# One core, two blocks in fp32 halves: GpSimd's two-operand passes on VectorE

## The chip, the cores and the metric

The kernel runs on one core of a Trainium2 chip as a single program. The metric is the device time of one execution in microseconds (us). Before the change the median of three runs is 1876.54 us (1874.93 to 1879.38).

A core has five engines, each with its own in-order stream of instructions, which wait for one another through semaphores: TensorE (PE: matmuls, and PEld: weight loads into the array), VectorE (DVE), ScalarE (ACT), GpSimd (POOL) and SyncE (SP, which here issues the transfers). SBUF is the on-chip memory, PSUM the matmuls' accumulator.

## The reference

One sequence of 256 tokens, 1024 channels, runs through two networks in a row, each of two layers, all in float32.

```python
# first block, per layer l
h = rmsnorm(x, norm1_g[l]) * (1 + sc1) + sh1
x = x + g1 * token_mix(h, ...)       # gated linear recurrence + latent attention, two branch gates
h = rmsnorm(x, norm2_g[l]) * (1 + sc2) + sh2
x = x + g2 * grouped_moe(h, ...)     # 16 experts of width 512, 2 per token
# the recurrence, chunks of 64 tokens, b = cumsum(log f), k = 1 - f
decay = exp(b[t] - b[s])             # t >= s
attn  = sum_d q[t] * decay * k[s]
# second block, per layer i (layer 0: windowed attention, layer 1: short convolution)
h = h + g1 * mixer(modulate(rms_norm(h, norm_mix[i]), sh1, sc1))
h = h + g2 * conv_ffn(modulate(rms_norm(h, norm_ffn[i]), sh2, sc2))   # width 2816
```

## The kernel before, in words

**Halves.** TensorE multiplies float32 in a rounded form (fp32r). To keep the precision, every operand is split into a high part and a rest: `split_to` (L515) has ScalarE copy a weight tile of 128x1024 to `hi` (L516), and VectorE or GpSimd subtract, `lo = w - hi` (L517). `mm3` (L534 to L537) then sends three matmuls per tile of 128x128: high by high, high weight by low activation, low weight by high activation. So a matmul of line L537 cannot start before its `lo` is there. `split_w` (L519) splits a loaded piece of 256 columns as two halves, by default the first `lo` on VectorE and the second on GpSimd (`engs=(V, G)`).

**Stages.** In order of time: token mix of layer 0 (0 to 325 us), its experts (to 603), token mix of layer 1 (to 895), its experts (to 1170), then the second block: windowed attention (to 1335), its feed-forward (to 1552), short convolution (to 1662), its feed-forward (to the end).

**Norms.** `norm_split` (L447) scales the activation with the norm and splits it in `hh` and `hl`. With the norm's scale given as `r`, VectorE makes `w = x * gain * r` (L454) for eight slices of 128x256, ScalarE adds the shift and rounds to `hh` (L458), VectorE takes the rest `hl` (L459). At a stage's start TensorE has nothing to do until these eight steps and the first weight halves are there. Otherwise the scale comes late: L474 multiplies by the gain, L492 by the norm.

**Token mix.** `forget`, `query`, `value`, `gate` (L643 to L712) project and make the recurrence's operands; GpSimd has two products in `query` (L681, L687). `states` transposes L687's result on TensorE (L720). `decays` (L737) makes six tiles `z` of 128x512 for the levels m = 2 to 64: a difference (L745: GpSimd for m = 4, 16, 64, VectorE for the others), two exponentials on ScalarE (L746, L747), and two products of 128x256 (L748 on VectorE, L749 on GpSimd). `recur` multiplies the tiles on TensorE (L765).

**Second block.** The query projections of the windowed attention turn their output by the rotary angles (L1574 to L1578: GpSimd has L1575). In `conv_ffn` the first two weight pieces of each feed-forward are split by GpSimd alone (`engs=(G, G) if g0 + s == 0`, L1776), all others by VectorE.

**What sets the order.** The program is written in one order, and a scheduler orders the instructions of each engine by priority and by its own estimate of when an engine is free. So a change of an engine moves other instructions too, on all engines but SP. `P` and `hlp` are pools of buffers in rotation: a raw weight tile is free for SP's next load when its split is done.

```python
513  def split_to(hi, lo, raw, lo_eng=None): ...
517      (lo_eng or V).tensor_tensor(lo, raw, hi.bitcast(F32), OP.subtract)
535      PE.matmul(ps, wh, ah, ...)      # hi by hi
536      PE.matmul(ps, wh, al, ...)      # hi by lo of the activation
537      PE.matmul(ps, wl, ah, ...)      # lo of the weight by hi
```

Of the kernel before, what the change touches and what calls it, by code (L numbers as in the profile page):

```python
# [108 lines left out]
def tile_kernel(ctx, tc, A, out, dbg=None, stop=None):  # L109
# [336 lines left out]
    def norm_split(x, gn, sh, pp, sp, w, hh=None, hl=None, before=None, late=None, r=None):  # L446

        if r is not None:
            for k in range(KD):
                if hh is None and k % 4 == 3:  # L450
                    G.tensor_tensor(w[k], x[:, k], r, OP.mult)
                    S.activation(w[k], w[k], AF.Identity, scale=gn[:, k:k + 1], bias=sh(k))
                    continue
                V.scalar_tensor_tensor(w[k], x[:, k], gn[:, k:k + 1], r, op0=OP.mult, op1=OP.mult)  # L454
                if hh is None:
                    S.activation(w[k], w[k], AF.Identity, bias=sh(k))
                else:
                    S.activation(hh[:, k], w[k], AF.Identity, bias=sh(k))  # L458
                    V.scalar_tensor_tensor(hl[:, k], w[k], sh(k), hh[:, k].bitcast(F32), op0=OP.add, op1=OP.subtract)  # L459
            return  # L460
# [30 lines left out]
        for k in range(KD):  # L491
            (G if k % 4 == 3 else V).tensor_tensor(w[k], w[k], r, OP.mult)  # L492
            if hh is None:
                S.activation(w[k], w[k], AF.Identity, bias=sh(k))
            else:
                S.activation(hh[:, k], w[k], AF.Identity, bias=sh(k))
                V.scalar_tensor_tensor(hl[:, k], w[k], sh(k), hh[:, k].bitcast(F32), op0=OP.add, op1=OP.subtract)
# [20 lines left out]

    def split_w(raw, hlp, kc, widths=(128, 128), engs=(V, G)):  # L519

        r, at = [], 0
        for i, n in enumerate(widths):
            hi, lo = pair(hlp, (kc, n))
            split_to(hi, lo, raw[:, :, at:at + n], engs[i])
            r.append((hi, lo))
            at += n
        return r
# [40 lines left out]
    def token_mix(l):  # L568
        key = (0, l)
        with ExitStack() as es:  # L570
# [64 lines left out]

            def proj(c0, s, engs=(V, V)):
                if s == 0 and c0 < 1024 and l:
                    engs = (G, G) if c0 else (V, G)
                w = pre.pop() if pre else split_w(load_w(w_in, 0, 8, c0 + 256 * s, 256), hlp, 8, engs=engs)
                return dense2(P, w, h, 8)  # L640
# [28 lines left out]
            def query(s):  # L669
# [10 lines left out]
                r.qi = H()  # L680
                G.tensor_tensor(r.qi, r.q, r.eb, OP.mult)  # L681
                kd = H()
# [3 lines left out]
                S.activation(kd, kd, AF.Exp, scale=-1.0)  # L686
                G.tensor_tensor(kd, kd, r.kk, OP.mult)  # L687
                r.kd = kd
# [48 lines left out]
            def decays(s):  # L737

                r = R[s]
                r.Z = []  # L740
                for m in (2, 4, 8, 16, 32, 64):
                    z = sp.tile([128, 2, T], F32, name=nm("z"), tag="z")
                    zb, bb, kb, qb = (x.rearrange("p h (c t) -> p (h c) t", t=m) for x in (z, r.b, r.kk, r.q))
                    n, mh = 2 * T // m, m // 2
                    (G if m in (4, 16, 64) else V).tensor_tensor(zb, bb, bb[:, :, mh - 1:mh].to_broadcast([128, n, m]), OP.subtract)  # L745
                    S.activation(zb[:, :, :mh], zb[:, :, :mh], AF.Exp, scale=-1.0)  # L746
                    S.activation(zb[:, :, mh:], zb[:, :, mh:], AF.Exp)  # L747
                    V.tensor_tensor(zb[:, :, :mh], zb[:, :, :mh], kb[:, :, :mh], OP.mult)  # L748
                    G.tensor_tensor(zb[:, :, mh:], zb[:, :, mh:], qb[:, :, mh:], OP.mult)  # L749
                    r.Z.append(z)  # L750
# [49 lines left out]
            def latents(s):  # L800
                ps = proj(2048, s, (V, V))
                for x in lat:
# [129 lines left out]
            def branch_gate(n, j):  # L932
                ps = proj(2720 + 1024 * j, n, (V, G))
                x_ = sig[n, j] = H()
# [528 lines left out]
    def win_attention(l, key):  # L1463
        with ExitStack() as es:
# [55 lines left out]
            for i in range(2):  # L1520
                split_to(*wv[i], raw[:, 4 * i:4 * i + 4], G if i else V)
            tc.cur_priority = tc.cur_priority + EARLY
# [3 lines left out]
            for k in range(KD):  # L1526
# [6 lines left out]
                if PAIR:  # L1533
                    (G if k < 4 else V).tensor_tensor(sq, sq, even, OP.add)
                with tc.issue_after(turned.ins):
# [16 lines left out]
            def bc2(x):  # L1552
                return x[:, None, :].to_broadcast([128, 2, T])
# [6 lines left out]
            def head_norm(ps, gcol, turn):  # L1560
# [11 lines left out]
                if turn:  # L1572
                    b_ = sp.tile([128, 2, T], F32, name=nm("rb"), tag="sq")
                    V.tensor_tensor(b_, p2, bc2(sinw), OP.mult)  # L1574
                    G.tensor_tensor(x, x, bc2(cosw), OP.mult)  # L1575
                    V.tensor_tensor(x, x, b_, OP.add)
# [34 lines left out]
            def wq(i):  # L1611
                return split_w(load_w(w_qkv, 0, 8, 256 * i, 256), hlp, 8, engs=(V, V))
            k1 = keys(1, hc)
# [121 lines left out]
    def conv_ffn(l, key):  # L1735
        with ExitStack() as es:
# [31 lines left out]
            for g0 in range(0, nb, 4):  # L1768
                n4 = min(4, nb - g0)
                for s in range(n4 // 2):  # L1770
# [4 lines left out]
                    for j, r in enumerate(rgu):  # L1775
                        ps = dense2(P, split_w(r, hlp, 8, engs=(G, G) if g0 + s == 0 else (V, V)), act(hh, hl), 8)  # L1776
                        y = sp.tile([128, 2, T], F32, name=nm("y"), tag="y")
# [98 lines left out]
```

## Time and profile before

| what | us |
|---|---|
| median of three runs | 1876.54 (1874.93 to 1879.38) |
| the profiled execution | 1876.0 |
| its span, first to last instruction | 1874.2 |
| PE busy in the span | 1727.8 (92%) |
| DVE busy | 1026.2 (55%) |
| ACT busy | 802.4 (43%) |
| POOL busy | 239.9 (13%) |

The profile is of one execution. An engine's busy time is the time in which it had an instruction under way; PE's matmuls overlap a little, and their ends are modelled. "L454 DVE" means line 454 of the kernel, run by VectorE. A number in brackets behind a row of the timeline is the idle time of that engine just before it, with the instruction that ended it. A wait is idle time of an engine, put down to the instruction whose end released it.

### The profile page before, as it was taken

The page shows a single profiled execution, that of the slowest core. Times are in us where ns is not written, and L with a number is a line of the kernel's source. Part 1 is how long each engine was busy: PE and PEld are TensorE (multiplying, and loading weights), DVE is VectorE, ACT ScalarE, POOL GpSimd, SP SyncE. Part 2 cuts the span into 40 slices and gives each one's busy share as a digit, 9 for nine tenths or more (in the row PEclk, how much of TensorE's full clock was granted, in tenths as well). Part 3 has the DMA queues.
Part 4 walks back from the last instruction along what each step waited for, and adds up shares of the span by engine and source line. Part 5 has one row for each costly group of instructions (what it writes and reads, how often), then busy time and mean ns, then how long its engine had stood idle before and what let it go on. Part 6 is the DMA issues. An engine that isn't in the chain of part 4 may idle for free. (4 is left out here: it accounts for less than half of the span.)

```text
span 1874.2 us, 30827 instructions
## 1 busy us (share of the span) xinstructions
PE 1727.8 (92%) x12555; PEld 1307.8 (70%) x12555; DVE 1026.2 (55%) x1838; ACT 802.4 (43%) x1460; POOL 239.9 (13%) x134
## 2 busy tenths in 40 slices
PE   6989998999999799999899988979899999989998
PEld 4777798444444777689444333857799997979998
DVE  4876555222222886555322222887576766678774
ACT  4544553111112553544211112767465554456663
POOL 1320232000000320223000000130200003430000
PEclk8999999899999899999899998999999999999999
DMA  9777894798799566896699997520587736576520
GB/s 319 250 259 258 293 328 158 283 392 318 290 391 368 181 204 240 292 324 216 240 386 392 392 387 260 165 91 1 193 300 272 246 114 202 181 267 228 180 91 23
DMA packets 277952, 467.33 MB, mean 249 GB/s; under 512 B 9282, under 2 KB 138288, under 8 KB 277728
## 3 DMA queue, kind: packets, MB, share of 16 engines
q1 hardware_dynamic: 276720, 462.76, 70.1%
q8 instruction: 143, 2.34, 0.5%
q10 hardware_dynamic: 656, 1.32, 0.2%
q14 instruction: 81, 0.66, 0.1%
q0 software_dynamic: 352, 0.23, 0.0%
HBM read 463.24 MB, written 1.05 MB: 248 GB/s over the span
## 5 line engine op out<-in xcount | busy, mean ns | idle before, releaser
L535 PE MATMUL mm<-hh,hi 128*128 128x256 f32 x1584 | 458.8, 290 | 11.1 <-ACT hh L458 5.7
L536 PE MATMUL mm<-hl,hi 128*128 128x256 f32 x1584 | 454.0, 287 | 9.5 <-DVE hl L459 7.7
L537 PE MATMUL mm<-hh,lo 128*128 128x256 f32 x1584 | 453.5, 286 | 4.6 <-DVE lo L517 4.6
L516 ACT CAST hi<-w 128x1024 fp32r<-128x1024 f32 (+4 forms) x330 | 309.6, 970 | 220.5 <-PE mm L536 178.4
L517 DVE TENSOR_TENSOR lo<-w,hi 128x1024 fp32r<-128x1024 f32 (+4 forms) x264 | 299.7, 1148 | 95.2 <-ACT hi L516 94.9
L517 POOL TENSOR_TENSOR lo<-w,hi 128x1024 fp32r<-128x1024 f32 x66 | 165.1, 2507 | 1275.7 <-ACT hi L516 1275.7
L535 PEld LDWEIGHTS mm<-hh,hi 128*128 128x128 f32 x1584 | 306.5, 194 | 26.2 <-ACT hh L458 8.4
L536 PEld LDWEIGHTS mm<-hl,hi 128*128 128x128 f32 x1584 | 307.0, 194 | 12.3 <-DVE hl L459 8.3
L537 PEld LDWEIGHTS mm<-hh,lo 128*128 128x128 f32 x1584 | 306.5, 193 | 7.8 <-DVE lo L517 5.4
L1194 PE MATMUL ps<-w,xg 128*64 128x512 f32 x512 | 231.7, 606 | 8.1 <-ACT xg L1166 5.7
L1195 PE MATMUL ps<-w,xg 128*64 128x512 f32 x512 | 231.5, 606 | 1.6 <-DMA w<-in_w_up_dram 1.6
L1194 PEld LDWEIGHTS ps<-w,xg 128*64 128x64 f32 x512 | 69.8, 139 | 149.1 <-issue 138.8
L1212 DVE TENSOR_TENSOR gx<-gx,ps 64x512 f32<-64x512 f32 (+1 forms) x35 | 23.4, 669 | 225.7 <-ACT gx L1211 187.1
L1211 ACT ACTIVATE gx<-ps 64x512 f32<-64x512 f32 (+1 forms) x35 | 20.0, 571 | 217.6 <-PE ps L1195 214.7
L1238 PE MATMUL ps<-w,he 128*64 128x512 f32 x240 | 110.7, 600 | 0.0
L1237 PE MATMUL ps<-w,he 128*64 128x512 f32 x240 | 110.0, 599 | 0.2 <-DMA w<-in_w_down_dram 0.2
L370 PE MATMUL ps<-w,crep 128*32 128x512 f32 x768 | 106.1, 605 | 3.4 <-DMA w<-in_ada_w_dram 2.0
L536 PE MATMUL yT<-zl,hi 128*128 128x256 f32 x352 | 99.1, 282 | 0.0
L535 PE MATMUL yT<-zh,hi 128*128 128x256 f32 x352 | 99.1, 281 | 0.0
L537 PE MATMUL yT<-zh,lo 128*128 128x256 f32 x352 | 99.0, 281 | 0.0
L535 PE MATMUL mm<-half,hi 128*128 128x256 f32 x320 | 93.0, 291 | 0.0
L536 PE MATMUL mm<-half,hi 128*128 128x256 f32 x320 | 91.2, 285 | 0.0
(468 smaller groups left out, 3014.5 us busy)
## 6 DMA issues: line engine op xcount, KB each, us to landing
w<-in_ada_w_dram SPq DMA_DIRECT2D x96, 1024.0 KB, 6.9
w<-in_w_gate_dram SPq DMA_DIRECT2D x64, 1024.0 KB, 14.5
w<-in_w_up_dram SPq DMA_DIRECT2D x64, 1024.0 KB, 16.2
w<-in_w_down_dram SPq DMA_DIRECT2D x64, 1024.0 KB, 12.7
w<-in_ffn_w_up_dram SPq DMA_DIRECT2D x44, 1024.0 KB, 5.3
w<-in_w_in_dram SPq DMA_DIRECT2D x36, 1024.0 KB, 8.7
w<-in_ffn_w_down_dram SPq DMA_DIRECT2D x22, 1024.0 KB, 6.8
w<-in_sc_w_in_dram SPq DMA_DIRECT2D x12, 1024.0 KB, 7.3
```

Source lines behind the costliest of these rows:

```text
L370: PE.matmul(ps[32 * g:32 * g + 32], crep[blk][:, 4 * s + g, SLOTS - 1 - i:SLOTS + 31 - i], w[i][s][:, g], start=(i + s == 0), stop=(i == n ...
L516: S.copy(hi, raw)
L517: (lo_eng or V).tensor_tensor(lo, raw, hi.bitcast(F32), OP.subtract)
L535: PE.matmul(ps, wh, ah, start=start, stop=False, skip_group_check=True)
L536: PE.matmul(ps, wh, al, start=False, stop=False, skip_group_check=True)
L537: latest[0] = PE.matmul(ps, wl, ah, start=False, stop=stop, skip_group_check=True).ins
L1194: PE.matmul(ps[0:64], xg[:, k, off:off + SL], wg[k // 4][:, k % 4], start=(k == 0), stop=(k == KD - 1), skip_group_check=True)
L1195: m = PE.matmul(ps[64:128], xg[:, k, off:off + SL], wu[k // 4][:, k % 4], start=(k == 0), stop=(k == KD - 1), skip_group_check=True)
L1211: S.activation(x_, ps[0:64], AF.Silu)
L1212: V.tensor_tensor(x_, x_, ps[64:128], OP.mult)
L1237: PE.matmul(py[0:64], he[:, j], cut(e, j, 0), start=(j == 0), stop=(j == 3), skip_group_check=True)
L1238: m = PE.matmul(py[64:128], he[:, j], cut(e, j, 1), start=(j == 0), stop=(j == 3), skip_group_check=True)
```

## The change

All two-operand passes that GpSimd ran go to VectorE: the 66 splits (L517), 24 products L749, 12 differences L745, four each of L681 and L687, five of L1575, two sums of L1534 and two of the norm's products L492; 119 instructions. GpSimd keeps its transfers. (The branch of `norm_split` that is deleted at L450 to L453 is never taken in this program.)

```diff
@@ norm_split
-                if hh is None and k % 4 == 3:
-                    G.tensor_tensor(w[k], x[:, k], r, OP.mult)
...
-            (G if k % 4 == 3 else V).tensor_tensor(w[k], w[k], r, OP.mult)
+            V.tensor_tensor(w[k], w[k], r, OP.mult)
@@ split_w
-    def split_w(raw, hlp, kc, widths=(128, 128), engs=(V, G)):
+    def split_w(raw, hlp, kc, widths=(128, 128)):
...
-            split_to(hi, lo, raw[:, :, at:at + n], engs[i])
+            split_to(hi, lo, raw[:, :, at:at + n])
@@ token mix: proj, query, decays, gates
-            def proj(c0, s, engs=(V, V)):
-                if s == 0 and c0 < 1024 and l:
-                    engs = (G, G) if c0 else (V, G)
+            def proj(c0, s):
...
-                G.tensor_tensor(r.qi, r.q, r.eb, OP.mult)
+                V.tensor_tensor(r.qi, r.q, r.eb, OP.mult)
...
-                G.tensor_tensor(kd, kd, r.kk, OP.mult)
+                V.tensor_tensor(kd, kd, r.kk, OP.mult)
...
-                    (G if m in (4, 16, 64) else V).tensor_tensor(zb, bb, bb[:, :, mh - 1:mh].to_broadcast([128, n, m]), OP.subtract)
+                    V.tensor_tensor(zb, bb, bb[:, :, mh - 1:mh].to_broadcast([128, n, m]), OP.subtract)
...
-                    G.tensor_tensor(zb[:, :, mh:], zb[:, :, mh:], qb[:, :, mh:], OP.mult)
+                    V.tensor_tensor(zb[:, :, mh:], zb[:, :, mh:], qb[:, :, mh:], OP.mult)
...
-                ps = proj(2720 + 1024 * j, n, (V, G))
+                ps = proj(2720 + 1024 * j, n)
@@ windowed attention
-                split_to(*wv[i], raw[:, 4 * i:4 * i + 4], G if i else V)
+                split_to(*wv[i], raw[:, 4 * i:4 * i + 4])
...
-                    (G if k < 4 else V).tensor_tensor(sq, sq, even, OP.add)
+                    V.tensor_tensor(sq, sq, even, OP.add)
...
-                    G.tensor_tensor(x, x, bc2(cosw), OP.mult)
+                    V.tensor_tensor(x, x, bc2(cosw), OP.mult)
@@ conv_ffn
-                        ps = dense2(P, split_w(r, hlp, 8, engs=(G, G) if g0 + s == 0 else (V, V)), act(hh, hl), 8)
+                        ps = dense2(P, split_w(r, hlp, 8), act(hh, hl), 8)
```

How the instructions move is shown at three places. In the changed kernel the line numbers are lower by four to seven: L450 and L455 are L454 and L459 of before, L513 is L517, L531 to L533 are L535 to L537, L739, L742, L743 are L745, L748, L749, L675, L678, L681 are L681, L684, L687, L700 is L706.

First VectorE at the start of the second block's first feed-forward (about 1336 us), before:

```order
L1690 SCALAR_TENSOR_TENSOR xT<-mm_26129,mod(1, 0)_190,xT 128x256 x2
L454 SCALAR_TENSOR_TENSOR wt_26212<-xT,gf_26210,rnorm 128x256 x2
L454 SCALAR_TENSOR_TENSOR wt_26213<-xT,gf_26210,rnorm 128x256 x2
L459 SCALAR_TENSOR_TENSOR hl_26209<-wt_26212,mod(1, 0)_190,hh_26208 128x256 x2
L459 SCALAR_TENSOR_TENSOR hl_26209<-wt_26213,mod(1, 0)_190,hh_26208 128x256 x2
L454 SCALAR_TENSOR_TENSOR wt_26214<-xT,gf_26210,rnorm 128x256 x2
```

and with the change:

```order
L1684 SCALAR_TENSOR_TENSOR xT<-mm_26129,mod(1, 0)_190,xT 128x256 x2
L513 TENSOR_TENSOR lo_26286<-w_26279,hi_26285 128x1024
L513 TENSOR_TENSOR lo_26290<-w_26279,hi_26289 128x1024
L513 TENSOR_TENSOR lo_26358<-w_26281,hi_26357 128x1024
L450 SCALAR_TENSOR_TENSOR wt_26212<-xT,gf_26210,rnorm 128x256 x2
L450 SCALAR_TENSOR_TENSOR wt_26213<-xT,gf_26210,rnorm 128x256
L455 SCALAR_TENSOR_TENSOR hl_26209<-wt_26212,mod(1, 0)_190,hh_26208 128x256 x2
```

Three of the four splits that POOL ran stand ahead of the norm's steps now; the fourth comes behind all sixteen of them.

Second, VectorE in the decays of token mix layer 1 (about 633 to 645 us), before:

```order
L745 TENSOR_TENSOR z_12725<-half_12511 128x512
L745 TENSOR_TENSOR z_12737<-half_12511 128x512
L745 TENSOR_TENSOR z_12749<-half_12511 128x512
L517 TENSOR_TENSOR lo_12804<-w_12801,hi_12803 128x1024
L676 SCALAR_TENSOR_TENSOR half_12522<-half_12522,half_12583 128x512
L748 TENSOR_TENSOR z_12725<-z_12725,half_12510 128x256
L684 TENSOR_TENSOR half_12592<-half_12511 128x512
L748 TENSOR_TENSOR z_12731<-z_12731,half_12510 128x128x2
```

and with the change:

```order
L670 SCALAR_TENSOR_TENSOR half_12522<-half_12522,half_12583 128x512
L742 TENSOR_TENSOR z_12725<-z_12725,half_12510 128x256
L675 TENSOR_TENSOR half_12590<-half_12522,half_12588 128x512
L678 TENSOR_TENSOR half_12592<-half_12511 128x512
L743 TENSOR_TENSOR z_12725<-z_12725,half_12522 128x256
L742 TENSOR_TENSOR z_12731<-z_12731,half_12510 128x128x2
L743 TENSOR_TENSOR z_12731<-z_12731,half_12522 128x128x2
L681 TENSOR_TENSOR half_12592<-half_12592,half_12510 128x512
```

The product L687 of before, which TensorE's transposes L720 wait for, stands as L681 seven instructions behind L676 (L670); ahead of these rows there are now four of L739 and no split, and `lo_12804` comes after four of the six levels.

Third, at the start of the last feed-forward (about 1664 us), VectorE with the change, with the end of the norm's steps and the splits behind them,

```order
L513 TENSOR_TENSOR lo_29908<-w_29901,hi_29907 128x1024
L450 SCALAR_TENSOR_TENSOR wt_29834<-xT,gf_29832,rnorm 128x256 x2
...
L455 SCALAR_TENSOR_TENSOR hl_29831<-wt_29837,mod(1, 1)_191,hh_29830 128x256 x2
L382 TENSOR_TENSOR mod(1, 1)_191<-ar_29894,cols 128x8
L382 TENSOR_TENSOR mod(1, 1)_191<-ar_29897,cols 128x8
L513 TENSOR_TENSOR lo_29912<-w_29901,hi_29911 128x1024
```

and TensorE there with the change:

```order
L531 MATMUL mm_29915<-hh_29830,hi_29907 128x256
L532 MATMUL mm_29915<-hl_29831,hi_29907 128x256
L533 MATMUL mm_29915<-hh_29830,lo_29908 128x256
L531 MATMUL mm_29915<-hh_29830,hi_29911 128x256
L532 MATMUL mm_29915<-hl_29831,hi_29911 128x256
L376 MATMUL ps_29889<-cst,a_29887 128x128 x4
L531 MATMUL mm_29987<-hh_29830,hi_29979 128x256
L533 MATMUL mm_29915<-hh_29830,lo_29912 128x256
```

Before, POOL made `lo_29912` beside the norm's steps; now it stands behind them on VectorE, and TensorE can send five matmuls of that product and L376 before it needs it. The order of SP's transfers is the same row by row.

## Rows read from the trace of the kernel before

**Rows 1.** The page: busy time of each engine, share of the span, instructions.

```profile
PE 1727.8 (92%) x12555; PEld 1307.8 (70%) x12555; DVE 1026.2 (55%) x1838; ACT 802.4 (43%) x1460; POOL 239.9 (13%) x134
```

**Rows 2.** The page: 40 slices of the span, POOL busy and DMA busy in tenths.

```profile
POOL 1320232000000320223000000130200003430000
...
DMA  9777894798799566896699997520587736576520
```

**Rows 3.** Groups by form, POOL: line, operation, shapes, count | busy us, mean ns | idle before.

```profile
L517 POOL TENSOR_TENSOR lo<-w,hi 128x1024 fp32r<-128x1024 f32 x66 | 165.1, 2507 | 1275.7 <-ACT hi L516 1275.7
L749 POOL TENSOR_TENSOR z<-z,half 128x256 f32<-128x256 f32 x24 | 25.4, 1085 | 5.3 <-ACT z L747 5.3
```

**Rows 4.** Groups by form, DVE.

```profile
L517 DVE TENSOR_TENSOR lo<-w,hi 128x1024 fp32r<-128x1024 f32 x226 | 284.9, 1272 | 79.0 <-ACT hi L516 78.9
...
L748 DVE TENSOR_TENSOR z<-z,half 128x256 f32<-128x256 f32 x24 | 18.8, 822 | 0.0
...
L454 DVE SCALAR_TENSOR_TENSOR wt<-xT,gf,rnorm 128x256 f32<-128x256 f32 x16 | 18.1, 1191 | 6.2 <-ACT rnorm L403 6.2
```

**Rows 5.** PE's waits over the whole span: us in total, times, longest.

```profile
PE mm L1645 <- ACT pw L1653: 10.4, 4, 8.6
...
PE mm L536 <- DVE hl L459: 7.7, 3, 4.7
PE ps L376 <- ACT a L373: 6.5, 5, 2.2
...
PE mm L535 <- ACT hh L458: 5.7, 2, 4.5
...
PE ps L720 <- POOL half L687: 5.1, 1, 5.1
```

**Rows 6.** Timeline, start of the first feed-forward: start, us, engine, line.

```profile
1336.86 9.68 POOL L517 TENSOR_TENSOR lo<-w,hi 128x1024 fp32r<-128x1024 f32 x4 [14.57 <-ACT hi L516]
```

```profile
1340.19 7.02 DVE L454 SCALAR_TENSOR_TENSOR wt<-xT,gf,rnorm 128x256 f32<-128x256 f32 x4 [3.10 <-ACT rnorm L403]
...
1348.72 1.66 DVE L454 SCALAR_TENSOR_TENSOR wt<-xT,gf,rnorm 128x256 f32<-128x256 f32 x4
```

**Rows 7.** Timeline, start of token mix layer 1: POOL, ACT, DVE, PE.

```profile
604.84 7.96 POOL L517 TENSOR_TENSOR lo<-w,hi 128x1024 fp32r<-128x1024 f32 x3 [296.67 <-ACT hi L516]
```

```profile
607.79 1.03 ACT L516 CAST hi<-w 128x1024 fp32r<-128x1024 f32 x1
```

```profile
610.53 3.35 DVE L454 SCALAR_TENSOR_TENSOR half<-xT,gn,rnorm 128x256 f32<-128x256 f32 x3
```

```profile
613.68 0.68 PE L535 MATMUL mm<-hh,hi 128*128 128x256 f32 x2 [4.50 <-ACT hh L458]
```

**Rows 8.** Timeline, decays of token mix layer 1: POOL, then PE.

```profile
642.57 1.44 POOL L687 TENSOR_TENSOR half<-half,half 128x512 f32<-128x512 f32 x1
643.98 3.50 POOL L749 TENSOR_TENSOR z<-z,half 128x256 f32<-128x256 f32 x3
```

```profile
653.72 1.50 PE L765 MATMUL lv<-z 128*128 128x128 f32 x12
```

**Rows 9.** Timeline, DVE in the second decays of layer 0, then of layer 1.

```profile
113.47 3.57 DVE L748 TENSOR_TENSOR z<-z,half 128x256 f32<-128x256 f32 x4
```

```profile
684.30 0.42 DVE L748 TENSOR_TENSOR z<-z,half 128x256 f32<-128x256 f32 x1
```

**Rows 10.** Timeline, query projections of the windowed attention: DVE, then POOL.

```profile
1223.51 2.88 DVE L1576 TENSOR_TENSOR xk<-xk,rb 128x512 f32<-128x512 f32 x1 [0.59 <-POOL xk L1575]
```

```profile
1243.30 1.71 POOL L1575 TENSOR_TENSOR xk<-xk,cst 128x512 f32<-128x512 f32 x1
```

**Rows 11.** Timeline, DVE at the start of the short convolution.

```profile
1554.92 6.41 DVE L474 TENSOR_SCALAR wt<-xT,gm 128x256 f32<-128x256 f32 x8
```

**Rows 12.** Timeline, DVE at the start of the last feed-forward.

```profile
1664.86 5.67 DVE L454 SCALAR_TENSOR_TENSOR wt<-xT,gf,rnorm 128x256 f32<-128x256 f32 x4 [3.10 <-ACT rnorm L403]
```

**Rows 13.** Busy time in ten stretches around the waits, the line of their sums.

```profile
sum 190.00, PE 141.42 PEld 110.22 DVE 162.49 ACT 114.23 POOL 102.10; mean PE 14.14 PEld 11.02 DVE 16.25 ACT 11.42 POOL 10.21
```

More of the change, by code (lines that the diff above doesn't have):

```diff
@@ L449, in norm_split @@
             for k in range(KD):
-                if hh is None and k % 4 == 3:
-                    G.tensor_tensor(w[k], x[:, k], r, OP.mult)
-                    S.activation(w[k], w[k], AF.Identity, scale=gn[:, k:k + 1], bias=sh(k))
-                    continue
                 V.scalar_tensor_tensor(w[k], x[:, k], gn[:, k:k + 1], r, op0=OP.mult, op1=OP.mult)
@@ L634, in token_mix @@
             h = act(hh, hl)
-            def proj(c0, s, engs=(V, V)):
-                if s == 0 and c0 < 1024 and l:
-                    engs = (G, G) if c0 else (V, G)
-                w = pre.pop() if pre else split_w(load_w(w_in, 0, 8, c0 + 256 * s, 256), hlp, 8, engs=engs)
+            def proj(c0, s):
+                w = pre.pop() if pre else split_w(load_w(w_in, 0, 8, c0 + 256 * s, 256), hlp, 8)
                 return dense2(P, w, h, 8)
@@ L800, in latents @@
             def latents(s):
-                ps = proj(2048, s, (V, V))
+                ps = proj(2048, s)
                 for x in lat:
@@ L1611, in wq @@
             def wq(i):
-                return split_w(load_w(w_qkv, 0, 8, 256 * i, 256), hlp, 8, engs=(V, V))
+                return split_w(load_w(w_qkv, 0, 8, 256 * i, 256), hlp, 8)
             k1 = keys(1, hc)
```

## The prediction, made before the changed kernel ran

> **What bounds the kernel now.** I read the page's busy times first. TensorE works 1727.8 of 1874.2 us, VectorE 1026.2, GpSimd 239.9 [rows 1]. So time can only be won where TensorE idles, about 146 us in all, and a stretch in which it is full gives nothing whatever the other engines do. The slices come next: GpSimd has work in four stretches alone, the two token mixes and, in the second block, the attention and around the short convolution; during the experts of either layer, where the transfers fill most of the time, its row shows zeros [rows 2]. Nothing of those 550 us is touched. Then the waits of TensorE: I looked for those that end on GpSimd, or on a VectorE or ScalarE step just behind something that shares its time with GpSimd. Five groups stand out [rows 5].
>
> What makes me look at VectorE's steps beside GpSimd's is one line at two times. At the start of the first feed-forward four L454 take 7.02 us on VectorE while GpSimd runs its four splits (1336.86 to 1346.54); a few microseconds later, GpSimd quiet, four L454 of the same shape take 1.66 us [rows 6]. So a step of 0.41 us becomes one of 1.76 while GpSimd works. The same shows at L748: 0.42 us alone [rows 9], 0.82 on the mean [rows 4], 0.89 in the second decays of layer 0 [rows 9].
>
> **What the work costs.** It leaves GpSimd: 66 splits of 2.51 us and 24 products of 1.09 [rows 3] and 29 smaller passes, near 234 of the 239.9 us. It arrives on VectorE at its prices: 66 splits at no more than 1.27 [rows 4] are 84 us; 24 L749, the same shape as L748, at 0.42 [rows 9] are 10; the 29 others, mostly of 128x512, twice L748's width, at about twice its price are near 22. That is up to 116 us more on VectorE. Against it stands what it loses by stretching. Bounds: nothing, if the steps are long for another reason; at most what the mean prices exceed the quiet ones by, for L748 24 x (0.82 - 0.42) = 10, for the sixteen L454 (1.19 - 0.41) x 16 = 12 [rows 4, 6], and for the 226 splits some tenth of a microsecond each, 23; with other lines like them I estimate 60. VectorE then ends near 1080 us of 1860: far from full on the mean. About 48 of the 66 splits are in stretches where TensorE is full, so I count them at nothing; what hides them is VectorE's idle time there, and should it run out, each would cost at most its 1.27 us. SP's order of transfers does not change, and GpSimd's queue keeps only transfers, which get nothing in front of them.
>
> **The sum, by place**, in order of size; each from the profiled execution.
>
> - *First feed-forward.* TensorE waits 4.7 us for the first `hl` [rows 5], because L454 runs 7.02 us [rows 6]. Now three splits (at most 3 x 1.27 = 3.8) stand in front. Their casts are early: GpSimd could start at 1336.86, so they are done about 1341, where the norm is ready at 1340.19; then three L454 of 0.41 and the first L459 end near 1342.6. `hl` came at 1347.6. That is -5.0. Bounds -5.4 (the whole difference of 7.02 and 1.66) and -3.5 (the fourth split, now behind sixteen steps, is late for the second product).
> - *Start of token mix 1.* GpSimd's three splits end at 604.84 + 7.96 = 612.80, the first L454 is held until then, TensorE starts 0.88 later, at 613.68 [rows 7]. Now four splits run on VectorE as their casts come; the last cast ends at 608.82 [rows 7], its split by 610.1, L454 by 610.5, and TensorE could start about 611. I take -3.0; bounds -4 and -2.
> - *The second decays* of both layers: VectorE reaches L706 late behind four L748 of 0.89 [rows 9], and TensorE waits up to 2.2 us for L373 each time [rows 5], which ScalarE does behind L706's sigmoid. With the change L706's counterpart stands behind three levels instead of all. -3.5 for both, bounds -4.4 (both waits gone) and -1.
> - *First decays of layer 1.* TensorE waits 5.1 us for L687 [rows 5], which GpSimd ends at 644.01 [rows 8]. On VectorE it follows L676 by seven instructions of 0.4 to 0.7 us and an exponential, near 639.5, so that wait goes almost whole. What is late next: the last tiles `z`, on GpSimd until 647.48 [rows 8], would come at about 647 from VectorE too, which has all twelve products and both sorts of differences to do; but L765, which needs them, stood at 653.72 [rows 8] behind other matmuls, and now stands before them. So TensorE waits again. -2.0, bounds -4 and +0.5. For the same decays of layer 0, where no single long wait stands, I take -1.0, bounds -3 and +1.5.
> - *Attention's queries.* L1576, a sum of the size of two L748, takes 2.88 us, and the last L1575 ends at 1245.01 [rows 10]; behind it lies the 8.6 us wait for L1653 [rows 5]. On VectorE a split of 1.27 and a product of 0.8 take the place of GpSimd's 2.51 and 1.71. -3.0, bounds -4 and -1.
> - *Short convolution.* Eight L474 take 6.41 us [rows 11], 0.80 each, and two L492 run on GpSimd. -2.0, bounds -3.5 and -0.5.
> - *Last feed-forward.* Four L454 take 5.67 us [rows 12], and TensorE's other two waits for `hl` (7.7 - 4.7 = 3.0) and the other for `hh` (5.7 - 4.5 = 1.2) are there [rows 5]. They go; but now `lo_29912` stands behind sixteen steps of 0.41 and one split: 1664.86 + 0.8 + 6.6 + 0.4 + 1.3 = 1674. TensorE has some six matmuls and L376 to send until then, where before it was released at 1664.86 + 5.67 + 0.45 = 1671. **+1.0**, bounds -0.5 and +2.
>
> Sum: -5.0 - 3.0 - 3.5 - 2.0 - 1.0 - 3.0 - 2.0 + 1.0 = -18.5 us; bounds -28.8 and -4.0. The profiled execution took 1876.0 us, 0.5 under the median of 1876.5. So 1857.5, and 1858 against the median.
>
> **The rivals.**
>
> *Absorbed by the experts' loads* (1867). The gains of both token mixes, 3.0 + 3.5 + 2.0 + 1.0 = 9.5 us, come ahead of stages whose slices show 9 tenths of the transfers [rows 2]. If the experts' first loads do not move up with the token mix, this part is lost: 1858 + 9 = 1867. For it: those stages hang on loads. Against it: in the slices ahead of them the transfers are not full, so loads are released by buffers that would come free sooner.
>
> *Slower: VectorE becomes the bound at these places.* Ten stretches around the waits, 190 us, hold 162.5 us of VectorE's work and 102.1 of GpSimd's [rows 13]. GpSimd's instructions there, counted in its timeline, are 18 splits, 24 L749 and 20 others: at VectorE's prices 18 x 1.27 + 24 x 0.42 + 20 x 0.8 = 49 us. If nothing of the 162.5 is stretch, VectorE needs 211 of 190 us, and the 21 us go to TensorE in the measure in which it waits for VectorE there; with half, 1876 + 10 = 1886. It decides at the point where a lone L748 or L454 stays at 0.8 or 1.2 us without GpSimd beside it; the four L454 of 1.66 us [rows 6] speak against it, as the forecast needs only some 22 of the 162.5 to be stretch for VectorE to fit in. The Trainium skill has the rule behind this rival, in "Perfetto Trace Analysis", section "Optimizing Scalar/DVE Operations": where VectorE is saturated, moving work off it to ScalarE, or even GpSimd, may help. By that rule these stretches, with VectorE at 86%, should lose by the change, and the time would be this rival's 1886. The same section adds that the two share a read port and that moving work between them might therefore not help, and the row of four L454 agrees with this half; no row shows the first half.
>
> *Late splits everywhere* (1872 or more, hardly to be told from no change). What the last feed-forward shows, a split behind the norm's steps, may turn up at the other starts too, as the scheduler orders by its own estimates. If 5.0 + 3.0 + 3.0 + 2.0 us of the starts and queries go, and the +1.0 becomes +2, there is -4.5 left, 1872; with the attention's start, which also gets two splits, a little less.
>
> *More* (1848). All the lower bounds of the places at once, -28.8: the waits go whole, and no new one comes at the last feed-forward.
>
> **How the numbers follow.** Forecast 0.57, more 0.14, absorbed 0.11, late splits 0.10, slower 0.08. A measurement of this kernel can tell about 0.2%, 3.7 us, from no change. The forecast's own range is 1850 to 1866; for 8 in 10 it reaches to 1846 below and takes in the absorbed case and part of the late splits, to 1872. Faster by over 0.2% (below 1872.8): 0.57 + 0.14 + 0.11 and a fifth of the late splits, 0.84; within 0.2%: the rest of the late splits, 0.08; slower: 0.08.
>
> **What would show it right or wrong.** VectorE's groups: L517 near 1.17 us or less, L748 and L454 near 0.42, L1576 near 0.7, its busy time 1050 to 1100 us in all. TensorE's wait for L720 and the 4.7 us for `hl` gone; at the last feed-forward one wait of about 5 us on L513. Wrong would be: L454 still over 1 us; waits of L533 on the splits L513 in other places; the experts' stage not starting earlier than before.

## The result, and the profile after

The changed kernel takes 1847.64 us (median of four runs, 1844.33 to 1850.55), the kernel before beside it 1876.92 (1874.93 to 1879.38): 0.984 times the time, with an interval of 0.9824 to 0.9856. The forecast was 1858, in a range of 1846 to 1872. The gain is 29 us where 18.5 were forecast; the time lies in that range, but below the narrower one, 1850 to 1866, that the prediction calls the forecast's own.

The profiled execution took 1850.5 us. Its page, busy time of each engine, and GpSimd's slices:

```profile
span 1848.7 us, 30656 instructions
...
PE 1728.0 (93%) x12555; PEld 1307.3 (71%) x12555; DVE 1014.7 (55%) x1957; ACT 801.9 (43%) x1460; POOL 6.0 (0%) x15
...
POOL 1000000000000000000000000000000000000000
```

Against [rows 1] GpSimd is empty, TensorE has the same work in a shorter span, and VectorE has 119 instructions more and **11.5 us less busy time**. The groups by form show how (instructions, busy us, mean ns of one, and idle time before them):

```profile
L513 DVE TENSOR_TENSOR lo<-w,hi 128x1024 fp32r<-128x1024 f32 x292 | 351.1, 1219 | 82.1 <-ACT hi L512 81.8
...
L742 DVE TENSOR_TENSOR z<-z,half 128x256 f32<-128x256 f32 x24 | 10.0, 418 | 0.0
...
L450 DVE SCALAR_TENSOR_TENSOR wt<-xT,gf,rnorm 128x256 f32<-128x256 f32 x16 | 6.8, 477 | 0.0
...
L976 DVE TENSOR_TENSOR half<-half,half 128x512 f32<-128x512 f32 x8 | 5.5, 683 | 0.0
L425 DVE TENSOR_TENSOR rnorm<-rnorm,sq 128x256 f32<-128x256 f32 x10 | 4.2, 422 | 0.7 <-ACT sq L423 0.3
L992 DVE TENSOR_TENSOR rnorm<-rnorm,sq 128x256 f32<-128x256 f32 x10 | 4.2, 420 | 0.4
```

The first three answer to L517, L748 and L454 of [rows 4]: L748 fell from 822 to 418 ns, L454 from 1191 to 477, and each is now near the price that [rows 6, 9] showed for it with GpSimd quiet. The last three are lines that I had not looked at. In the same view of the kernel before they stood so:

```profile
L982 DVE TENSOR_TENSOR half<-half,half 128x512 f32<-128x512 f32 x8 | 18.7, 2332 | 0.0
...
L998 DVE TENSOR_TENSOR rnorm<-rnorm,sq 128x256 f32<-128x256 f32 x10 | 12.2, 1222 | 1.0 <-ACT sq L996 0.4
L425 DVE TENSOR_TENSOR rnorm<-rnorm,sq 128x256 f32<-128x256 f32 x10 | 10.2, 1022 | 1.5 <-ACT sq L423 1.0
```

L425 and L998 add up the squares for a norm, ahead of a stage's start: 14 of their 22.4 us were stretch.

TensorE's waits after the change (engine and line, what it waited for, us in all, times, the longest):

```profile
PE mm L1639 <- ACT pw L1647: 7.7, 3, 6.7
...
PE mm L531 <- ACT hi L512: 6.5, 4, 4.2
...
PE ps L1268 <- issue: 5.3, 3, 3.0
```

The last line answers to this one of before:

```profile
PE ps L1274 <- issue: 4.6, 3, 2.3
```

Of [rows 5], the waits for L720 and for L459's first `hl` are gone, and that for L1653 (L1647 now) is down to 6.7. Two waits are new or longer, both met again below: 4.2 us for a cast on ScalarE, at the last feed-forward, and 3.0 us in TensorE's own queue, in the experts of layer 0, where the longest was 1.1 before. In the experts of layer 1 that second one fell from 2.3 us to 1.1, so its sum is nearly what it was. Three places of the forecast in the timeline (start, duration, engine, line, count, and in brackets the idle time before): the norm of token mix 1 with TensorE's first matmul, its decays, and the norm of the first feed-forward:

```profile
611.40 1.27 DVE L450 SCALAR_TENSOR_TENSOR half<-xT,gn,rnorm 128x256 f32<-128x256 f32 x3
...
612.48 0.51 PE L531 MATMUL mm<-hh,hi 128*128 128x256 f32 x2 [0.52 <-ACT hh L454]
...
636.47 0.68 DVE L681 TENSOR_TENSOR half<-half,half 128x512 f32<-128x512 f32 x1
...
637.59 0.60 PE L714 MATMUL ps<-cst,half 128*128 128x128 f32 x4
...
1325.04 1.27 DVE L450 SCALAR_TENSOR_TENSOR wt<-xT,gf,rnorm 128x256 f32<-128x256 f32 x3
```

Three steps take 1.27 us there, where four took 7.02 [rows 6]. The product that GpSimd ended at 644.01 [rows 8] (L687, now L681) ends at 637.15, and the transposes behind it start without a wait.

**Where the 25 us of the profiled executions went.** I paired the same ScalarE and VectorE instructions of both traces and took how far their starts moved (the median in each stretch, us):

| up to the end of | shift so far | in this stretch | forecast |
|---|---|---|---|
| token mix 0, first decays | -3.5 | -3.5 | -1.0 |
| token mix 0, second decays | -7.2 | -3.7 | -1.75 |
| experts of layer 0 | +0.7 | **+7.9** | 0 |
| token mix 1, start | -1.2 | -1.9 | -3.0 |
| token mix 1, first decays | -6.3 | -5.1 | -2.0 |
| token mix 1, second decays | -10.4 | -4.1 | -1.75 |
| experts of layer 1 | -11.8 | -1.4 | 0 |
| attention with its queries | -15.7 | -3.9 | -3.0 |
| first feed-forward, start | -22.4 | -6.7 | -5.0 |
| short convolution | -26.0 | -3.6 | -2.0 |
| last feed-forward | -25.0 | +1.0 | +1.0 |

Without the experts the places give -31.5, where -18.5 were forecast. Between the places, where TensorE is full (the gates, the bodies of the feed-forwards), the shift does not move at all.

### The profile page after: what moved, and what is told of

It reads as the page before. It is cut to its first block, busy times and chain, and to the rows that moved or that the text cites. A ratio compares the mean times of both kernels' runs of the same rounds, so it can differ in the third digit from the quotient of the medians.

```text
span 1848.7 us, 30656 instructions
## 1 busy us (share of the span) xinstructions
PE 1728.0 (93%) x12555; PEld 1307.3 (71%) x12555; DVE 1014.7 (55%) x1957; ACT 801.9 (43%) x1460; POOL 6.0 (0%) x15
## 5 line engine op out<-in xcount | busy, mean ns | idle before, releaser
L531 PE MATMUL mm<-hh,hi 128*128 128x256 f32 x1584 | 457.8, 289 | 10.3 <-ACT hi L512 5.1
L533 PE MATMUL mm<-hh,lo 128*128 128x256 f32 x1584 | 452.5, 286 | 1.7 <-DVE lo L513 1.6
L513 DVE TENSOR_TENSOR lo<-w,hi 128x1024 fp32r<-128x1024 f32 (+4 forms) x330 | 365.8, 1125 | 98.3 <-ACT hi L512 97.7
L512 ACT CAST hi<-w 128x1024 fp32r<-128x1024 f32 (+4 forms) x330 | 310.0, 971 | 246.0 <-PE mm L532 193.8
L531 PEld LDWEIGHTS mm<-hh,hi 128*128 128x128 f32 x1584 | 305.4, 193 | 23.2 <-ACT hi L512 7.9
L533 PEld LDWEIGHTS mm<-hh,lo 128*128 128x128 f32 x1584 | 305.4, 193 | 4.4 <-DVE lo L513 2.3
L531 PE MATMUL yT<-zh,hi 128*128 128x256 f32 x352 | 99.1, 281 | 0.0
L533 PE MATMUL yT<-zh,lo 128*128 128x256 f32 x352 | 99.0, 281 | 0.0
L531 PE MATMUL mm<-half,hi 128*128 128x256 f32 x320 | 93.1, 291 | 0.0
L533 PE MATMUL mm<-half,lo 128*128 128x256 f32 x320 | 90.5, 283 | 0.0
## 6 DMA issues: line engine op xcount, KB each, us to landing
w<-in_w_down_dram SPq DMA_DIRECT2D x64, 1024.0 KB, 12.8
```

Of the source, the lines that this page charges most:

```text
L512: S.copy(hi, raw)
L531: PE.matmul(ps, wh, ah, start=start, stop=False, skip_group_check=True)
L533: latest[0] = PE.matmul(ps, wl, ah, start=False, stop=stop, skip_group_check=True).ins
```

## The experiments

The theory: the time comes from VectorE's two-operand steps, which GpSimd's passes stretch. The rivals: VectorE is simply the quicker engine for these passes; the order of the instructions matters, not the engine; one kind of pass does it all.

**e1: the change, and GpSimd still at work.** VectorE does all passes as in the change; GpSimd does passes of the same sizes again (those of 128x512 in two pieces, so 161 instructions in all), with results that nobody reads.

```diff
+    def ghost(a):
...
+            G.tensor_tensor(o, x, x, OP.mult)
...
+    def both(o, a, b, op, g):
+        V.tensor_tensor(o, a, b, op)
+        ghost(g)
...
+        if lo_eng is G:
+            G.tensor_tensor(raw, raw, hi.bitcast(F32), OP.mult)
...
-                    G.tensor_tensor(zb[:, :, mh:], zb[:, :, mh:], qb[:, :, mh:], OP.mult)
+                    both(zb[:, :, mh:], zb[:, :, mh:], qb[:, :, mh:], OP.mult, zb[:, :, mh:])
```

> The changed kernel's orders on VectorE, TensorE and ScalarE are kept row by row; GpSimd runs 119 passes of the old sizes again behind VectorE's, with results that nothing reads (each split's raw tile is overwritten after use; the smaller ones are written to a scratch tile, those of 128x512 in two pieces). Theory A (stretch: a VectorE step with two SBUF inputs runs longer while GpSimd runs such a pass): L454's and L748's counterparts rise from 0.42-0.48 us to 0.7 or more, VectorE's busy time rises from 1015 by 50 to 110 us, and the time rises by 10 to 25 us over the changed kernel's 1848, to 1858 to 1873. Rival B (the gain came only from GpSimd's own slow results being waited for): nobody waits for GpSimd here, VectorE's durations stay, 1845 to 1851.

Measured: 1896.69 us (three of the four executions took 1893.96 to 1897.38), 1.0093 (1.0063 to 1.0123) times before: 49 more than the change alone, and more than the theory's own range. The page and two groups (L465 and L765 answer to L450 and L742):

```profile
PE 1741.5 (92%) x12555; PEld 1314.0 (69%) x12555; DVE 1097.2 (58%) x1957; ACT 804.0 (42%) x1460; POOL 264.9 (14%) x161
...
L465 DVE SCALAR_TENSOR_TENSOR wt<-xT,gf,rnorm 128x256 f32<-128x256 f32 x16 | 13.1, 866 | 0.0
...
L765 DVE TENSOR_TENSOR z<-z,half 128x256 f32<-128x256 f32 x24 | 12.6, 525 | 0.1
```

VectorE has the same 1957 instructions in the same order as in the change and is busy 82.5 us longer. VectorE's being the quicker engine is therefore not what the gain is made of: with that alone, the kernel is slower than before. A doubt stays: these passes also hold buffers, so part of the 49 could be loads that start later. e5 and e6 are about that.

**e2 and e3: one kind alone.** e2 moves the 66 splits, e3 the 53 other passes.

```diff
# e2
-    def split_w(raw, hlp, kc, widths=(128, 128), engs=(V, G)):
+    def split_w(raw, hlp, kc, widths=(128, 128), engs=(V, V)):
# e3
-                    G.tensor_tensor(zb[:, :, mh:], zb[:, :, mh:], qb[:, :, mh:], OP.mult)
+                    V.tensor_tensor(zb[:, :, mh:], zb[:, :, mh:], qb[:, :, mh:], OP.mult)
```

> The kernel before with only its 66 splits moved to VectorE; decays, products and norms stay on GpSimd. By the places in the two traces: first feed-forward -6.7, start of token mix 1 -2, short convolution some -2.5, attention -1 to -2, last feed-forward +1: about -12 us, 1862 to 1868. If the splits carried the whole gain: 1848; if only the small passes do: 1877.

> The kernel before with only the 53 smaller passes moved (decays, query products, rotary products, norm products); the 66 splits stay on GpSimd. The four decays -3.5, -3.5, -5, -4.4, the attention's queries about -2, short convolution -1: about -18 us, 1855 to 1862. Together with the splits alone this should add to the whole change's -29 within 4 us; if one part only uncovers the other's wait, the two sum to much less than -29.

Measured: e2 1866.32, 0.9933 (0.9907 to 0.996), inside what was expected; e3 1863.06, 0.9927 (0.9904 to 0.9951), just outside. By the map of shifts e2 gains at the starts (-6.7 at the first feed-forward, -2.6 at the short convolution) and nothing in token mix 0 (+1.9); e3 gains in the decays (-6.5 in token mix 0). Against the kernel before beside them (1877.13) they gain 10.8 and 14.1, together 24.9 of the 29.3. That is 4.4 short, where I had allowed 4, and less than the width of either interval: neither does it all, and neither needs the other.

**e4: 32 splits stay on GpSimd**, those of the gates, the branches' up projections and the output projections, where TensorE is full.

```diff
-                wab = split_w(rab, hlp, 8)
+                wab = split_w(rab, hlp, 8, engs=(V, G))
```

> The changed kernel, but 32 splits (branch gates, the branches' up projections, the output projection: stretches in which TensorE is full) stay on GpSimd. If work in stretches with a full TensorE is worth nothing: 1845 to 1851, as the changed kernel, with VectorE's L517 of about 1.5 us beside them. If the stretch costs there too: 1853 or more.

Measured: 1850.6, 0.9857 (0.9834 to 0.9879), not to be told from the change. GpSimd's group, and two of VectorE's:

```profile
L517 POOL TENSOR_TENSOR lo<-w,hi 128x1024 fp32r<-128x1024 f32 x32 | 80.3, 2510 | 780.3 <-DMA w<-in_ada_w_dram 440.9 <-ACT hi L516 339.3
```

```profile
L982 DVE TENSOR_TENSOR half<-half,half 128x512 f32<-128x512 f32 x8 | 18.7, 2332 | 0.0
...
L998 DVE TENSOR_TENSOR rnorm<-rnorm,sq 128x256 f32<-128x256 f32 x10 | 12.2, 1222 | 1.0 <-ACT sq L996 0.4
```

80.3 us of GpSimd's work cost nothing that shows in the time, where TensorE is full. The two lines of VectorE are exactly as long as before the change; in the change they are down to 683 and 420 ns. So some 21 us of VectorE's stretch stay in e4, and the time does not notice them. VectorE's splits stood at 1234 ns on the mean; how long those beside GpSimd's took, of which I had expected 1.5 us, this mean does not tell.

**e5 and e6: what of a GpSimd pass does the harm.** Both do the change's work on VectorE, and after each of the 66 moved splits GpSimd touches the raw weight tile, which is dead by then. In e5 it reads two operands and writes; in e6 it writes only.

```diff
# e5
+        if lo_eng is G:
+            G.tensor_tensor(raw, raw, hi.bitcast(F32), OP.mult)
# e6
+        if lo_eng is G:
+            G.memset(raw, 0.0)
```

> As the run with GpSimd's copies of all passes, but with those of the 66 splits alone: after VectorE's split GpSimd multiplies the dead raw tile by the high half in place (reads and writes SBUF). The orders of the other engines are those of the changed kernel. Theory A (GpSimd's reading passes stretch VectorE's steps): from the map of the first such run, whose feed-forward starts, short convolution and attention lost most, +22 to +36 us over the changed kernel, 1870 to 1884. Rival C (it was the small pieces in the decays that cost): within 5 us of the changed kernel.

> The same 66 places, but GpSimd only writes: it sets the dead raw tile to zero, reading nothing. The tile is held as long as GpSimd needs, so the loads see the same kind of delay. If the stretch comes from GpSimd's reads: VectorE's L454 stays near 0.48 us and the time within 4 us of the changed kernel, 1844 to 1852. If any GpSimd work does it, or the later release of the raw tiles: 1860 or more, in proportion to GpSimd's busy time.

Measured: e5 1883.72, 1.0035 (1.002 to 1.0051); e6 1849.1, 0.9857 (0.9828 to 0.9885). Page and groups of e5:

```profile
PE 1732.4 (92%) x12555; PEld 1310.0 (70%) x12555; DVE 1078.1 (57%) x1957; ACT 804.4 (43%) x1460; POOL 183.8 (10%) x81
...
L519 POOL TENSOR_TENSOR w<-w,hi 128x1024 f32<-128x1024 f32 x66 | 177.8, 2696 | 1502.8 <-DVE lo L517 773.7 <-DMA cst<-in_tables_dram 586.6 <-DMA w<-in_ada_w_dram 49.9
...
L454 DVE SCALAR_TENSOR_TENSOR wt<-xT,gf,rnorm 128x256 f32<-128x256 f32 x16 | 13.1, 864 | 0.0
```

and of e6:

```profile
PE 1719.7 (93%) x12555; PEld 1300.3 (71%) x12555; DVE 1017.3 (55%) x1957; ACT 802.1 (44%) x1460; POOL 68.9 (4%) x81
...
L519 POOL MEMSET w<- 128x1024 f32 x66 | 62.9, 952 | 1574.5 <-DVE lo L517 849.5 <-DMA cst<-in_tables_dram 590.1 <-DMA w<-in_ada_w_dram 48.9
...
L454 DVE SCALAR_TENSOR_TENSOR wt<-xT,gf,rnorm 128x256 f32<-128x256 f32 x16 | 6.8, 478 | 0.0
```

The timelines at the first feed-forward's norm, of e5 and then of e6:

```profile
1336.65 5.74 POOL L519 TENSOR_TENSOR w<-w,hi 128x1024 f32<-128x1024 f32 x2 [1.16 <-DVE lo L517]
...
1337.63 5.44 DVE L454 SCALAR_TENSOR_TENSOR wt<-xT,gf,rnorm 128x256 f32<-128x256 f32 x3
```

```profile
1319.67 1.27 DVE L454 SCALAR_TENSOR_TENSOR wt<-xT,gf,rnorm 128x256 f32<-128x256 f32 x3
...
1319.86 0.95 POOL L519 MEMSET w<- 128x1024 f32 x1 [0.40 <-POOL w L519]
```

In e5 three L454 take 5.44 us beside a pass that reads, about as long as GpSimd's two; in e6 three take 1.27 with a writing pass inside them. e6 holds the raw tiles as well, so the loss of e5 is not the mere presence of a second user of the buffer; what e6 leaves open is that its passes are shorter, 62.9 us in all beside e5's 177.8. TensorE's waits answer that: those that a transfer ended come to 11.4 us in the changed kernel, 12.8 in e1, 12.4 in e5 and 11.7 in e6, so hardly more than one of the 49 and 36 us by which e1 and e5 take longer than the change is a late load. The Trainium skill states the rule in "SBUF — State Buffer", section "Who interferes with whom": a VectorE instruction with two inputs in SBUF contends with a GpSimd instruction that reads SBUF, not with one that only writes it; the shared port is an exclusive lock, and the order of issue decides which of the two blocks. The rows agree, with 864 against 478 ns.

**e7 and e8: the new wait at the last feed-forward.** The changed kernel, with the first two weight pieces of each feed-forward ranked 40 (e7) or 100 (e8) places further ahead for the scheduler.

```diff
-                        ps = dense2(P, split_w(r, hlp, 8), act(hh, hl), 8)
+                        with early(40 if g0 + s == 0 else 0):
+                            ws = split_w(r, hlp, 8)
+                        ps = dense2(P, ws, act(hh, hl), 8)
```

> The changed kernel, with the first feed-forward pieces' splits 40 steps earlier in the scheduler's priority. At the last feed-forward the second split then stands before the last two L454 instead of behind all sixteen steps. TensorE's wait there, 4.2 us for L512's cast and 0.3 for the split, shrinks by about 1.5: 1845 to 1848, hardly to be told from the changed kernel.

> The same by 100 steps: the second split and the casts stand ahead of the norm's steps at the last feed-forward. L454 starts some 1.2 us later, and the wait of 4.2 us goes: -3 us, 1842 to 1847 against the changed kernel's 1848. If the later L454 costs as much as the wait gave, no change.

Measured: e7 1846.42, 0.9821 (0.9793 to 0.9849); e8 1843.55, 0.9818 (0.9795 to 0.984). Neither can be told from the change by its time alone. In the waits of that stretch the 4.2 us become 2.2 in e7. In e8 the wait for a cast is gone, and this is left:

```profile
PE mm L537 <- DVE lo L517: 0.8, 2, 0.6
PE mm L536 <- DVE hl L459: 0.3, 1, 0.3
```

**e9: layer 0's decays and query products stay on GpSimd**, to see whether the experts behind them swallow their gain.

```diff
-                    G.tensor_tensor(zb[:, :, mh:], zb[:, :, mh:], qb[:, :, mh:], OP.mult)
+                    (V if l else G).tensor_tensor(zb[:, :, mh:], zb[:, :, mh:], qb[:, :, mh:], OP.mult)
```

> The changed kernel, but the decays and query products of the first layer's token mix stay on GpSimd (its splits move). In the changed kernel that token mix ends 7.2 us earlier and the experts behind it give some 8 us back, with 3 us or more in which TensorE waits in its own queue. If the experts of layer 0 absorb what comes before them: the token mix is 7 us longer, the experts lose nothing, and the time is that of the changed kernel, 1845 to 1851. If the loss in the experts has nothing to do with it: 1853 to 1857.

Measured: 1853.87, 0.9853 (0.9828 to 0.9877). That is the side on which the experts do not swallow it, but its interval reaches over the change's. Token mix 0 gains nothing here (+0.4), and the experts of layer 0 still lose, 2.4 us up to their middle and 4.2 in all, where they lost 7.9 in the change. But the repeat of the changed kernel (e10), with the early start, lost 3.9 in its experts of layer 0, so these executions do not show that any of the loss goes with the early start.

**e10 and e11: the changed kernel and e8 again**, side by side.

> The changed kernel itself, on the same chip as the two others of this set: 1844 to 1851.

> The changed kernel with the first feed-forward pieces' splits 100 steps earlier, again and in more rounds: 2 to 4 us below the changed kernel beside it, 1841 to 1847. If the first look was chance: no difference.

Measured: 1850.26, 0.9845 (0.9818 to 0.9872), and 1845.53, 0.9823 (0.9798 to 0.9848). Twice e8's kernel came out 4 to 5 us below the changed one. The intervals overlap, so the gain is likely, not sure; that its wait is gone is shown. It is the best version of this study.

## Why the prediction was right

**The mechanism held.** L454 and L748 fell to the prices of a quiet GpSimd, as the forecast took from [rows 6, 9], and e1, e5 and e6 show the cause: a reading GpSimd pass beside them.

**Nothing for work under a full TensorE.** Held: 48 splits were counted at nothing; e4 leaves 32 of those on GpSimd, and its time cannot be told from the change.

**The term of the sum that was mis-sized is the next wait in the decays.** For token mix 1's first decays the forecast let TensorE wait again, since the last tiles `z` "would come at about 647 from VectorE too", and so kept 2.0 of the 5.1 us; with the three other decays it took 6.5. In the changed kernel the last product for a `z` ends at 643.89, and L759 (L765 of before) does not wait for it; what is left is 0.9 us for a cast:

```profile
643.48 0.41 DVE L743 TENSOR_TENSOR z<-z,half 128x256 f32<-128x256 f32 x1
```

```profile
643.75 0.39 PE L531 MATMUL mm<-hh,hi 128*128 128x256 f32 x1 [0.90 <-ACT hi L512]
...
644.63 1.50 PE L759 MATMUL lv<-z 128*128 128x128 f32 x12
```

The four decays gave 16.4 us, 9.9 of the 13.0 by which the places exceed the forecast. They gave what TensorE's waits there held, or more: 5.1 us where it waited 5.1 for L687, 3.7 and 4.1 where it waited 2.2 each time for L373, and 3.5 in token mix 0's first decays, where four waits for splits, 4.6 us together, became one of 1.3.

**VectorE's stretch was mis-sized too**, "with other lines like them I estimate 60", and so its busy time, forecast at 1050 to 1100. Had all its stretch stayed, VectorE would hold the work of before, 1026.2, and the moved passes: 66 x 1.22 + 24 x 0.42 + some 19 = near 109 us. It held 1014.7, so **about 120 us** of stretch went. Of the lines that I priced, two came near their bounds of 10 and 12 (L748 8.8, L454 11.3), and the splits reached 13 of 23 (busy time of VectorE's own instructions of before, less that of as many after). The other lines were taken at 15 and were near 87, among them the norms' sums L425 and L998 with 14, L982 with 13 and the 26 L444 with 7.5. The view of [rows 4] holds them too, and I did not look for them. But this is not what made the places larger: in e4 L982 and L998 keep their stretch at no cost, and at the first feed-forward the shift stays between -15.7 and -16.0 all through L425 and moves only with L454, to -20.9 at the first L459. At the short convolution it stays at -22.4 through L474, which the forecast named first, and moves with L492 and L497.

**The places.** Seven of nine came out larger than forecast, the start of token mix 1 smaller (-1.9 for -3.0; TensorE starts 1.2 us earlier where token mix 0's lead is already lost).

**The last feed-forward** gave the +1.0 forecast, and that is luck: it came by another release. The forecast named `lo_29912`, late behind sixteen steps on VectorE. The trace shows 4.2 us for the cast `hi` on ScalarE (L512), which stands behind the last of the norm's `hh` (L454) there, and 0.3 for the split behind it; the waits of 3.0 and 1.2 that the forecast named are gone:

```profile
1644.90 0.91 ACT L454 ACTIVATE hh<-wt,mod(1, 1)_191 128x256 fp32r<-128x256 f32 x2 [1.07 <-DVE wt L450]
1645.71 2.92 ACT L512 CAST hi<-w 128x1024 fp32r<-128x1024 f32 x3
...
1646.79 0.58 PE L531 MATMUL mm<-hh,hi 128*128 128x256 f32 x1 [4.16 <-ACT hi L512]
...
1647.66 0.58 PE L533 MATMUL mm<-hh,lo 128*128 128x256 f32 x1 [0.29 <-DVE lo L513]
```

The step that failed there is that I followed the order of VectorE alone; the cast that the split needs comes after all eight `hh`, though ScalarE has idle time of 1.07 us ahead of the last two. e8 moves cast and split forward, and the wait goes.

**The rivals.** "Slower" fell at the point named for it: a lone L748 takes 418 ns and a lone L454 477. The Trainium skill's rule in "Perfetto Trace Analysis", section "Optimizing Scalar/DVE Operations", has two halves. By the first, moving work off a saturated VectorE may help; here stretches with VectorE at 86% gained from getting more work. The second, that the shared port may undo a move between the two, agrees with what was measured (864 against 478 ns in e5 and e6). "Late splits" turned up at one place. "Absorbed" is half true at most: the experts of layer 0 gave back 7.9 us in this execution and 3.9 in its repeat, but also 4.2 in e9, where they started no earlier; those of layer 1 gave back nothing. "More" (1848) is what the time comes to, but by larger gains at the places and a loss that it did not have.

## What to carry to other kernels

Compare one line's shortest and mean duration, for every line of an engine, before pricing a move: a line whose mean is two or three times its shortest may be paying for another engine that runs beside it, and the sum of those differences (here 120 us on VectorE against GpSimd's 240 of work) is what silencing that engine gives back in busy time. In the kernel's time only that part counts which stands where TensorE waits: here 29 us. A second engine's help is worth its place only where its passes lie beside nothing that shares their path; where TensorE is full they cost nothing and bring nothing. And when a step moves, follow what it needs (here the cast on ScalarE) in the new order as well as the step itself.

## What was not expected of the hardware

**A step beside a reading pass does not run slower: it stands until the pass has ended.** e5 shows it on a step of 128x4, which takes 0.15 us a little later (at 817.42):

```profile
814.48 2.40 POOL L519 TENSOR_TENSOR w<-w,hi 128x1024 f32<-128x1024 f32 x1 [5.48 <-DVE ar L380]
```

```profile
814.52 2.37 DVE L382 TENSOR_TENSOR mod(1, 0)_190<-ar,cols 128x4 f32<-128x4 f32 x1
```

The pass ends at 816.88, the step at 816.89. In the kernel before, each of VectorE's steps that took over 1.5 times the shortest of its group, and 0.2 us more, ends a fixed time after a GpSimd pass: those with two inputs 0.28 us after it for 128x256, 0.55 for 128x512, 1.08 for 128x1024. So a pass costs what is left of it when the step comes, whatever the step's own size.

**VectorE steps with one SBUF input are stretched too, those that read PSUM are not.** Two groups of e1, which stood at 690 and 287 ns before the change:

```profile
L952 DVE TENSOR_SCALAR half<-mm 128x512 f32<-128x512 f32 x16 | 11.0, 689 | 19.8 <-PE mm L552 19.6
...
L928 DVE TENSOR_SCALAR p<-p,sm 128x128 f32<-128x128 f32 x16 | 9.0, 563 | 0.5
```

`mm` is in PSUM, `p` in SBUF. Of the sixteen `p` two make the difference, with 2.49 and 2.50 us; the others stay at 0.29. Of L952's counterpart in the kernel before (L935) four lie whole inside a GpSimd pass, and take 690 to 692 ns. A pass that only writes holds up these one-input steps as well, unlike those with two inputs. In e6:

```profile
213.35 0.95 POOL L519 MEMSET w<- 128x1024 f32 x1 [10.76 <-DVE sm L911]
```

```profile
213.35 1.17 DVE L913 TENSOR_SCALAR p<-p,sm 128x128 f32<-128x128 f32 x2
...
214.62 0.55 DVE L913 TENSOR_SCALAR p<-p,sm 128x128 f32<-128x128 f32 x2
```

Two steps take 1.17 us beside the pass, the next two 0.55. e6 has only five such steps, so its time does not show them.

**TensorE waits in its own queue in the experts, and its clock is lower there.** In the changed kernel, and from the windows of the same trace (PE, PEld, DVE, ACT, POOL busy us; granted clock; DMA share; GB/s):

```profile
455.79 1.53 PE L1268 MATMUL ps<-PT,y 64*128 64x256 f32 x16 [3.01 <-issue]
...
474.00:476.00 2.00, 1.37 (x18) 0.28 (x8) 0.08 (x1) 0.47 (x1) 0.00 (x0) 0.50 0.00 0
```

The same 60 us in the kernel before, the changed one and its repeat (e10):

```profile
425.00:485.00 60.00, 53.82 (x422) 26.30 (x419) 18.31 (x52) 12.79 (x30) 0.00 (x0) 0.94 0.70 255
```

```profile
425.00:485.00 60.00, 51.14 (x378) 25.55 (x376) 15.18 (x41) 11.34 (x27) 0.00 (x0) 0.83 0.58 211
```

```profile
425.00:485.00 60.00, 50.46 (x386) 24.59 (x386) 15.19 (x41) 11.15 (x26) 0.00 (x0) 0.89 0.57 207
```

"issue" is time in which TensorE waits for nothing that the profile shows. It stands at the scatter L1268 behind a branch. In the experts of layer 0 its longest was 1.1 us before the change, 1.8 and 2.0 in e9 and e2, whose token mix 0 ends no earlier, and 2.8 to 4.7 in all the others, whose token mix 0 ends 1.2 us or more earlier. In the experts of layer 1 it goes the other way, from 2.3 us before to 1.1. The traces also hold the transfers of instructions: in all 13 of them each such wait of over 0.8 us in the experts, 42 in number, ends 1.3 to 1.7 us after one of 16 KB on queue q8 has ended, however long the wait. In the wait above that transfer runs from 453.28 to 454.41. So the queue most likely waits for its instructions, and what moves the wait is when they come; no run varied this.

The clock is mixed from two levels, 1.00 (2.4 GHz) and 0.50 (1.2 GHz), in every execution; in these 60 us its mean fell from 0.94 to 0.83, in the repeat to 0.89. As an estimate, with TensorE taken as full, that is 60 x 0.11 = 6.6 us and 60 x 0.05 = 3.0 of work at full clock, where the experts of layer 0 lost 7.9 and 3.9. Why the clock differs between executions of one kernel stays open.
